# A two-layer gated parallel encoder on one core: order of the first loads, padded probabilities in D0, weight loads issued from the Pool queue

## The chip, the core and the metric

The kernel runs on one core of one Trainium2 chip. The core has a matrix engine (TensorE, "PE" in the rows; its weight loads are "PEld"), a vector engine (DVE), a scalar engine (ACT), GpSimd (POOL) and a sync engine (SP), each with an instruction queue of its own that is worked off in order. DMAs are issued by instructions in these queues and run on 16 DMA engines. The metric is the time of one execution in device microseconds; lower is better.

## What is computed

512 tokens of width 1024 go through two layers. Each layer normalises its input, projects it with one wide matrix, runs four attention branches (A: window with sink, B: differential, C: dense with rotary positions, D: three dilated groups), gates each branch, projects it back, mixes the four with sigmoid weights and adds the result to its input:

```python
for l in range(DEPTH):
    h = _rmsnorm(x, norm_gain[l])
    p = _project(h, w_in[l])                     # a_q, a_k, ..., d_v, gate, merge
    ...
    oa = _window_sink_attention(qa, ka, va, bias_a, sink[l]...)
    ob = _diff_attention(qb, kb, vb, tbl_b, lam, lam_init, sub_norm_gain[l])
    oc = _dense_gqa(qc, kc, vc)
    od = _dilated_attention(qd, kd, vd, bias_d)  # groups (128,1), (512,4), (2048,16)
    for n, o in enumerate((oa, ob, oc, od)):
        gated = o * silu(gate[n])
        merged += sigmoid(merge[n]) * (gated @ w_branch[l, n])
    x = x + merged @ w_out[l]
```

## The kernel before

Every float32 product is made from two float16 halves: an operand is split into a high part (`..h`, `whi`, `ph`, made on ACT) and a low part (`..l`, `wlo`, `pl`, made on DVE from the operand and the high part), and three matmuls (high by high, high by low, low by high) add up in PSUM.

The weights lie in DRAM as 132 pieces of 1 MB in the order in which they are used (`ORDER`). `dma_w` (L118) brings a piece as two loads of 128 x 1024 float32 into staging buffers `wst` (three of them), `load_w` splits it into one of four `whi`/`wlo` pairs (L142 on ACT, L143 on DVE), and `take_w` keeps three pieces ahead (`AHEAD`). A piece feeds 48 matmuls of 512 columns (`proj_n`, L396 to L398; `proj_t`, L407 to L409).

A layer is a chain of attention generators, each woven (`weave`) with the projections of what comes next. An attention step has `scores` (products `s`, L560 and L561; the bias is added on DVE into `t`; exponential and split into `ph`, `pl`) and `values` (products `pv`, L565 to L567). Tiles come from pools with a fixed number of buffers per tag, and a scheduler that replays the program on a timeline of its own fixes the order of each engine's queue when the kernel is built.

Opening of the program: `load_x` brings four blocks of 128 tokens (`xt`), `norm_a` normalises a block, `norm_b` transposes it on TensorE and splits it into `hT_h`, `hT_l`. The fourth block goes through `norm_t` instead, which splits first and transposes by two DMAs. `bias_lines` (L260) makes the relative-position bias of all heads: a matmul of the table `rb` with the one-hot matrix `oh` (97 x 2432), copied into `acc` rows 0 to 7 (L276, L278), and then one DMA on SP writes 23 copies of these 8 rows to `lines` in DRAM (L929). `load_bias` reads skewed tiles back from `lines` before each attention; the first of them are `bias_a`.

In group 0 of branch D (`attn_d0`, L801) a block of 128 keys meets only 256 queries, 64 on either side, so `ph` and `pl` hold 256 columns per key block and `values` multiplies them in pieces: 64-query halves (`lo`, `hi`) and, for the two middle blocks, one 128-query piece; 12 groups of three matmuls per head.

Of the kernel before, what the change touches and what calls it, by code (L numbers as in the profile page):

```python
# [85 lines left out]
)  # L86
PIECE = 128 * 2048
AHEAD = 3


@with_exitstack
def encoder(ctx, tc, x, wf, norm_gain, qk_gain, sink, lambda_vec, sub_gain, rel_bias, onehot, rope, out):
# [83 lines left out]
    def load_x(src, tt):  # L176
        if tt % 2 == 0:
            x_sb[tt // 2] = qk.tile([128, 2, D], F32, tag="qx", name="xt", bufs=2)
        nc.sync.dma_start(out=x_sb[tt // 2][:, tt % 2, :], in_=src[tt * 128:tt * 128 + 128, :])

    gain_b = {}

# [16 lines left out]
    load_x(x, 0)  # L199
    load_gain(0)  # L200
    dma_w(0)
    load_x(x, 1)
    with tc.issue_after(dma_w(1).ins):
        load_x(x, 2)
        nc.sync.dma_start(out=rb, in_=bass.AP(tensor=rel_bias.tensor, offset=rel_bias.offset, ap=[[0, 3], [36, 32], [1, 36]]))
        nc.sync.dma_start(out=oh, in_=onehot)
        load_x(x, 3)

    def norm_a(l, tt):

        xt = x_sb[tt // 2][:, tt % 2, :]
        ss = sm.tile([128, 2], F32, tag="n_ss", name="ss")
        for j in range(2):
            sq = tmp.tile([128, 512], F32, tag="sq", name="sq")
            S.activation(sq, xt[:, 512 * j:512 * j + 512], AF.Square, accum_out=ss[:, j:j + 1])
        V.tensor_tensor(ss[:, 0:1], ss[:, 0:1], ss[:, 1:2], op=ALUa)
        ln = sm.tile([128, 1], F32, tag="n_ln", name="ln")
        S.activation(ln, ss[:, 0:1], AF.Ln, scale=1.0 / D, bias=eps_x)
        rs = sm.tile([128, 1], F32, tag="n_rs", name="rs")
        S.activation(rs, ln, AF.Exp, scale=-0.5)  # L220
        hs = []
        for j in range(2):
            f = slice(512 * j, 512 * j + 512)
            h = tmp.tile([128, 512], F32, tag="gs", name="h", bufs=4)
            V.scalar_tensor_tensor(h, xt[:, f], rs, gain_b[l][:, f], op0=ALUm, op1=ALUm)
            hs.append(h)
        return hs

    def norm_b(tt, hs):

        for j in range(2):
            tr = transpose4(hs[j])
            d = slice(4 * j, 4 * j + 4)
            c = slice(tt * 128, tt * 128 + 128)
            S.activation(hT_h[:, d, c], tr, AF.Copy, scale=SH)
            done = V.scalar_tensor_tensor(hT_l[:, d, c], tr, SH, hT_h[:, d, c], op0=ALUm, op1=ALUs)
        return done

    def norm_t(tt, hs):

        hi = tmp.tile([128, 2, 512], F16, tag="st", name="h_hi", bufs=3)
        lo = tmp.tile([128, 2, 512], F16, tag="st", name="h_lo", bufs=3)
# [17 lines left out]
    def bias_lines():  # L260
# [3 lines left out]
        for a in (32, 64):  # L264
            r = slice(a, a + 32)
            V.tensor_tensor(rb[r, :], rb[r, :], rb16[r, :], op=ALUs)
            V.tensor_copy(rb16[r, :], rb[r, :])
        V.tensor_tensor(rb16[64:96, :], rb[64:96, :], rb16[64:96, :], op=ALUs)
        for i, (s0, ln_, h0, nh, off, w) in enumerate(SEG.values()):
            for e in range(0, ln_, 512):  # L270
                n = min(512, (ln_ + 1 - e))
                c = slice(s0 + e, s0 + e + n)
                p = ps_mm.tile([128, 512], F32, tag="mm", name="p")
                PE.matmul(p[:8, :n], rb16[:, h0:h0 + 8], oh[:, c], start=True, stop=True)
                if i % 2:
                    S.activation(accf[0:8, c], p[:8, :n], AF.Copy, scale=1.0 / SB)  # L276
                else:
                    V.tensor_scalar(accf[0:8, c], p[:8, :n], 1.0 / SB, None, op0=ALUm)  # L278
# [165 lines left out]
    def proj_q(res, l, kind, col, perm=False):  # L444
# [4 lines left out]
        for tt in range(NT):  # L449
# [9 lines left out]
            st = tmp.tile([128, 4, 4, HD], F16, tag="st", name="st", bufs=3)  # L459
# [10 lines left out]
    def proj_k(res, l, kind, col, perm=False):  # L470
# [6 lines left out]
        for tt in range(NT):  # L477
            p = proj_n(w, tt, perm, 512)
            rs_of(p, 8, out_ap=rsk[:, tt, :])
            kg = tmp.tile([128, 512], F32, tag="qn", name="kg")  # L480
            V.tensor_tensor(heads(kg), heads(p), tabs[l][:, n:n + 1, :].to_broadcast([128, 8, HD]), op=ALUm)
            st = tmp.tile([128, 16, 128], F16, tag="st", name="st", bufs=3)
            hi = st[:, 0:8, 0:HD]
            S.activation(hi, heads(kg), AF.Copy, scale=KS)
            V.scalar_tensor_tensor(st[:, 8:16, 0:HD], heads(kg), KS, hi, op0=ALUm, op1=ALUs)
            V.tensor_copy(st[:, :, HD:128], st[:, :, 0:HD])
            nc.sync.dma_start_transpose(out=kk[:, :, tt * 128:tt * 128 + 128], in_=st.rearrange("p a d -> p (a d)"))
            yield

    VS = SV / PROJ  # L490
# [20 lines left out]
    def proj_kv(res, l, kind, col):  # L511
# [6 lines left out]
        for tt in range(NT):  # L518
# [7 lines left out]
            st = tmp.tile([128, 4, 128], F16, tag="st", name="st", bufs=3)  # L526
# [270 lines left out]
    def attn_d0(l, qs, kk, rsk, v):  # L797
        bias, o, n12 = {}, {}, {}

        def scores(h):  # L800
            if h % 4 == 0:  # L801
                bias[h // 4] = load_bias("D0", h, 4, "bias_d0")
            ph, pl = new_p()
            for kb in range(4):
                q0, q1 = max(128 * kb - 64, 0), min(128 * kb + 192, T)
                n, f0 = q1 - q0, q0 - (128 * kb - 64)
# [2 lines left out]
                s_mm(p, kk[:, h, ks], kk[:, 8 + h, ks], qs[:, h, q0:q1])  # L809
                t = at.tile([128, 512], F32, tag="t", name="t", bufs=3)[:, :n]  # L810
                V.scalar_tensor_tensor(t, p, rsk[:, kb, h:h + 1], bias[h // 4][:, h % 4, f0:f0 + n], op0=ALUm, op1=ALUa)  # L811
                f = slice(f0, f0 + n)
                probs(t, n, nm[:, l, 12 + h:13 + h], ph[:, kb, f], pl[:, kb, f])
            return ph, pl

        def values(h, pp):
# [6 lines left out]
                                  in_=dsc[2][hp].rearrange("(t p) e -> p t e", p=128))  # L823
            pv = ps_pv.tile([128, 4, 66], F32, tag="pv", name="pv")
            for qb in range(4):
                vt = [v[:, k, h] for k in range(4)]
                lo, hi = pv[0:64, qb, 0:65], pv[64:128, qb, 0:65]
                if qb > 0:
                    k = qb - 1
                    pv_mm(lo, ph[:, k, 192:256], pl[:, k, 192:256], vt[k], HD, True, False)  # L830
                if qb < 3:
                    k = qb + 1
                    pv_mm(hi, ph[:, k, 0:64], pl[:, k, 0:64], vt[k], HD, True, False)
                if qb == 0:
                    pv_mm(lo, ph[:, 0, 64:128], pl[:, 0, 64:128], vt[0], HD, True, True)
                    pv_mm(hi, ph[:, 0, 128:192], pl[:, 0, 128:192], vt[0], HD, False, True)
                elif qb == 3:
                    pv_mm(lo, ph[:, 3, 64:128], pl[:, 3, 64:128], vt[3], HD, False, True)
                    pv_mm(hi, ph[:, 3, 128:192], pl[:, 3, 128:192], vt[3], HD, True, True)
                else:  # L840
# [74 lines left out]
    for l in range(L):  # L915
# [5 lines left out]
        if l:  # L921
            norm_t(3, last)
        else:
            bias_lines()
            with tc.issue_after(normed.ins):
                gain_tables(0)
        run(qa, proj_kv(r, l, "A", 512))
        if l == 0:
            nc.sync.dma_start(out=lines.rearrange("c h n -> h c n"),  # L929
                              in_=accf[0:8, 0:LINE].unsqueeze(1).to_broadcast([8, COPIES, LINE]))  # L930
            with tc.issue_after(normed.ins):
                setup_columns()
                setup()
        weave(attn_a(l, r["qA"], *r["kA"], r["vA"]),
# [90 lines left out]
```

## Time and profile before

| | us |
|---|---|
| time before, median of 3 runs | 1674.26 (1674.24 to 1674.72) |
| the profiled execution, own time | 1674.46 |
| its span, first to last instruction | 1672.4 |
| outside the span | 2.1 |
| mean granted TensorE clock over the span | 0.985 of 2.4 GHz |

The page of the profile gives busy time per engine; the rows that the prediction rests on stand two sections below. A busy PE means that some matmul is in flight: matmuls overlap, so the time that one costs is read from the distance between two starts in the timeline, not from its duration. DVE and ACT instructions overlap a little at their ends too, so that busy time in a window is less than the sum of durations.

### The profile page before, as it was taken

What the parts mean: (1) busy time and instruction counts of PE and PEld (TensorE: products, weight loads), DVE (VectorE), ACT (ScalarE), POOL (GpSimd) and SP (SyncE); (2) the same over time, 40 slices, a digit from 0 to 9 for tenths busy, and PEclk for the clock granted to TensorE, in tenths of its full rate; (3) what the DMA queues carried; (4) which work ended last, traced back from release to release, by engine and by line L of the source; (5) the groups of instructions that cost most, each with busy time, mean ns of one, the idle gap of its engine ahead of it and who ended that gap; (6) DMA issues with size and microseconds to landing.
All of it is one profiled execution on the core that took longest, in us unless ns stands there. A gap on an engine that the chain in (4) does not pass through costs nothing.

```text
span 1672.4 us, 26438 instructions
## 1 busy us (share of the span) xinstructions
PE 1602.6 (96%) x10302; PEld 834.6 (50%) x10302; DVE 1075.9 (64%) x2104; ACT 961.0 (57%) x1771; POOL 8.8 (1%) x32
## 2 busy tenths in 40 slices
PE   3389999999999999999999999999999999999999
PEld 1155545564555554454445554556455555445444
DVE  3368866785576766575556887678457676657451
ACT  3157676566664656564545767556667464556450
POOL 1000000000000000000000000000000000000000
PEclk8699999999999999999999999999999999999999
DMA  5974733352356757435357483336235674753421
GB/s 188 97 161 133 164 109 95 100 133 76 110 121 155 183 144 191 141 114 143 109 169 173 105 183 119 93 101 133 76 98 130 152 180 132 200 146 94 133 88 51
DMA packets 230817, 218.37 MB, mean 131 GB/s; under 512 B 176316, under 2 KB 188620, under 8 KB 230509
## 3 DMA queue, kind: packets, MB, share of 16 engines
q1 hardware_dynamic: 229925, 214.26, 50.0%
q0 software_dynamic: 768, 2.43, 0.5%
q8 instruction: 80, 1.31, 0.3%
q14 instruction: 44, 0.36, 0.1%
HBM read 163.94 MB, written 10.24 MB: 104 GB/s over the span
## 4 chain that ended last, share of the span: by engine, by line
PE 89%; DMA 6%; DVE 3%; ACT 1%; issue 0%; SPq 0%; DVEq 0%; ACTq 0%
PE mm L396 15%; PE mm L397 15%; PE mm L398 15%; PE mm L407 10%; PE mm L409 10%; PE mm L408 10%; PE s L560 3%; PE s L561 3%; PE pv L565 3%; DMA hT_h<-h_hi 2%; PE pv L567 2%; PE pv L566 2%; DMA oh<-in_onehot_dram 1%; DMA wst<-in_wf_dram 1%; DMA qs<-st 1%; DVE wlo L143 1%
## 5 line engine op out<-in xcount | busy, mean ns | idle before, releaser
L396 PE MATMUL mm<-whi,hT_h 128*128 128x512 f16 (+1 forms) x1408 | 522.7, 371 | 38.7 <-DMA hT_h<-h_hi 31.1
L397 PE MATMUL mm<-wlo,hT_h 128*128 128x512 f16 (+1 forms) x1408 | 522.6, 371 | 0.7 <-DVE wlo L143 0.7
L398 PE MATMUL mm<-whi,hT_l 128*128 128x512 f16 (+1 forms) x1408 | 522.2, 371 | 1.2 <-DMA hT_l<-h_lo 1.2
L143 DVE SCALAR_TENSOR_TENSOR wlo<-wst,whi 128x1024 f16<-128x1024 f32 (+1 forms) x260 | 307.3, 1204 | 203.1 <-ACT whi L142 202.0
L142 ACT ACTIVATE whi<-wst 128x1024 f16<-128x1024 f32 (+1 forms) x260 | 262.6, 1036 | 269.4 <-PE mm L408 122.3
L396 PEld LDWEIGHTS <-hT_h 128*128 128x128 f16 x1408 | 144.4, 103 | 175.9 <-DMA hT_h<-h_hi 32.1
L398 PEld LDWEIGHTS <-hT_l 128*128 128x128 f16 x1408 | 144.4, 103 | 147.6 <-issue 2.6
L397 PEld LDWEIGHTS <-hT_h 128*128 128x128 f16 x1408 | 144.4, 103 | 146.4 <-issue 7.7
L407 PE MATMUL mm<-hT_h,whi 128*128 128x512 f16 x512 | 194.1, 379 | 0.0
L409 PE MATMUL mm<-hT_h,wlo 128*128 128x512 f16 x512 | 194.1, 379 | 0.0
L408 PE MATMUL mm<-hT_l,whi 128*128 128x512 f16 x512 | 194.0, 379 | 0.0
L551 ACT ACTIVATE t<-t,nm 128x512 f32<-128x512 f32 (+2 forms) x224 | 132.0, 599 | 69.1 <-DVE t L811 24.1
L556 DVE TENSOR_TENSOR pl<-t,ph 128x512 f16<-128x512 f32 (+2 forms) x224 | 119.1, 543 | 37.8 <-ACT ph L555 36.5
L565 PE MATMUL pv<-v,ph 128*128 128x65 f16 (+2 forms) x992 | 123.8, 202 | 0.1
L566 PE MATMUL pv<-v,ph 128*128 128x64 f16 (+2 forms) x992 | 122.9, 201 | 0.0
L567 PE MATMUL pv<-v,pl 128*128 128x65 f16 (+2 forms) x992 | 121.0, 199 | 0.0
L409 PEld LDWEIGHTS <-wlo 128*128 128x128 f16 x768 | 75.1, 98 | 88.9
L407 PEld LDWEIGHTS <-whi 128*128 128x128 f16 x768 | 75.1, 98 | 87.1
L408 PEld LDWEIGHTS <-whi 128*128 128x128 f16 x768 | 75.1, 98 | 86.6
L555 ACT ACTIVATE ph<-t 128x512 f16<-128x512 f32 (+2 forms) x224 | 110.9, 506 | 2.8 <-PE pv L567 0.7
L560 PE MATMUL s<-qs,kk 128*128 128x512 f16 (+4 forms) x384 | 99.4, 293 | 1.7 <-DVE gs L582 1.3
L561 PE MATMUL s<-qs,kk 128*128 128x512 f16 (+4 forms) x384 | 100.5, 292 | 0.0
(173 smaller groups left out, 1925.4 us busy)
## 6 DMA issues: line engine op xcount, KB each, us to landing
wst<-in_wf_dram SPq DMA_DIRECT2D x264, 512.0 KB
dsc<-num SPq DMA_DIRECT2D x16, 260.0 KB
xt<-in_x_dram SPq DMA_DIRECT2D x8, 512.0 KB
bias_b<-lines SPq DMA_DIRECT2D x8, 448.0 KB
bias_a<-lines SPq DMA_DIRECT2D x16, 192.0 KB
num<-dsc SPq DMA_DIRECT2D x8, 260.0 KB
n<-dsc SPq DMA_DIRECT2D x8, 260.0 KB
bias_d<-lines SPq DMA_DIRECT2D x32, 64.0 KB
```

The source lines that it names most:

```text
L142: S.activation(hi[:, a], st[:, e:e + step], AF.Copy if sc is SW else AF.Identity, scale=sc)
L143: V.scalar_tensor_tensor(lo[:, a], st[:, e:e + step], sc, hi[:, a], op0=ALUm, op1=ALUs)
L396: PE.matmul(p[:, :ncol], a, wh, start=(k == 0), stop=False)
L397: PE.matmul(p[:, :ncol], a, wl, start=False, stop=False)
L398: PE.matmul(p[:, :ncol], b, wh, start=False, stop=(k == 7))
L407: PE.matmul(p, wh[:, k, f], rh[:, k], start=(k == 0), stop=False)
L408: PE.matmul(p, wh[:, k, f], rl[:, k], start=False, stop=False)
L409: PE.matmul(p, wl[:, k, f], rh[:, k], start=False, stop=(k == nk - 1))
L561: PE.matmul(p, klo, q, start=False, stop=True)
L565: PE.matmul(o, ph, vt[:, 0:d + 1], start=start, stop=False)
L566: PE.matmul(o[:, 0:d], ph, vt[:, d + 2:2 * d + 2], start=False, stop=False)
L567: PE.matmul(o, pl, vt[:, 0:d + 1], start=False, stop=stop)
```

## The change

Three things are done together.

First, the opening. SP issues only the four `xt` blocks and the gain; the first weight pieces go out beside them. `rb` and `oh` are loaded later and from Pool, behind a small Pool copy (`there`) that waits for the fourth `xt` block. All four blocks take `norm_b`. `bias_lines` moves behind the key and value projection of branch A; its matmul has each head's column repeated 16 times (`rbr`), so that the bias lands in all 128 rows of `acc` (16 copies of 8 heads), and two DMAs from Pool, of 128 and of 56 rows, write the 23 copies.

Second, D0. `ph` and `pl` hold 384 columns per key block, with 64 zeroed columns on either side (four Pool memsets per head), and `values` uses 128-query pieces alone, as branch A does: 10 groups of three matmuls per head.

Third, the weights. `dma_w` issues on Pool (`nc.gpsimd`), and there are five `wst` buffers. The staging tag `st` gets four buffers, and `proj_k` splits its tile and its transposing DMA in two.

```diff
+WST = 5
@@ dma_w
-            st = wp.tile([128, 1024], F32, tag="wst", name="wst", bufs=3)
-            dma = nc.sync.dma_start(out=st, in_=src[:, e:e + 1024])
+            st = wp.tile([128, 1024], F32, tag="wst", name="wst", bufs=WST)
+            dma = nc.gpsimd.dma_start(out=st, in_=src[:, e:e + 1024])
@@ first loads
-    load_x(x, 1)
-    with tc.issue_after(dma_w(1).ins):
-        load_x(x, 2)
-        nc.sync.dma_start(out=rb, in_=...)
-        nc.sync.dma_start(out=oh, in_=onehot)
-        load_x(x, 3)
+    dma_w(1)
+    for tt in range(1, NT):
+        load_x(x, tt)
+    there = const.tile([128, 1], F32, name="there")
+    tables = G.tensor_copy(there, x_sb[1][:, 1, 0:1])
@@ bias_lines
+        rbr = const.tile([97, len(SEG), 128], F16, name="rbr")
+            V.tensor_copy(rbr[:, i].rearrange("p (c h) -> p c h", h=8),
+                          rb16[:, h0:h0 + 8].unsqueeze(1).to_broadcast([97, 16, 8]))
-                PE.matmul(p[:8, :n], rb16[:, h0:h0 + 8], oh[:, c], start=True, stop=True)
+                PE.matmul(p[:, :n], rbr[:, i], oh[:, c], start=True, stop=True)
-                    S.activation(accf[0:8, c], p[:8, :n], AF.Copy, scale=1.0 / SB)
+                    S.activation(accf[:, c], p[:, :n], AF.Copy, scale=1.0 / SB)
+        for c0, c1_ in ((0, 16), (16, COPIES)):
+            nc.gpsimd.dma_start(out=lines[c0:c1_]..., in_=accf[0:8 * (c1_ - c0), 0:LINE])
     for tt in range(NT):
-        normed = (norm_b if tt < 3 else norm_t)(tt, norm_a(0, tt))
-        if tt < 2:
-            load_w(tt)
+        normed, split = norm_b(tt, norm_a(0, tt))
+        if tt == 0:
+            with tc.issue_after(scaled[0].ins):
+                load_w(0)
+            with tc.issue_after(split.ins):
+                load_w(1)
@@ proj_k
-            st = tmp.tile([128, 16, 128], F16, tag="st", name="st", bufs=3)
+            st = [tmp.tile([128, 8, 128], F16, tag="st", name="st", bufs=4) for _ in range(2)]
...
+            for i in range(2):
+                V.tensor_copy(st[i][:, :, HD:128], st[i][:, :, 0:HD])
+                nc.sync.dma_start_transpose(out=kk[:, 8 * i:8 * i + 8, ...], in_=st[i]...)
@@ attn_d0 scores
+            for pp in (ph, pl):
+                G.memset(pp[:, :, 0:64], 0.0)
+                G.memset(pp[:, :, 320:384], 0.0)
-                f = slice(f0, f0 + n)
+                f = slice(f0 + 64, f0 + 64 + n)
@@ attn_d0 values
-                if qb > 0:
-                    pv_mm(lo, ph[:, k, 192:256], pl[:, k, 192:256], vt[k], HD, True, False)
...
-                    pv_mm(pv[:, qb, 0:65], ph[:, qb, 64:192], pl[:, qb, 64:192], vt[qb], HD, False, True)
+                kbs = [k for k in (qb - 1, qb, qb + 1) if 0 <= k < 4]
+                for kb in kbs:
+                    f = slice((qb - kb + 1) * 128, (qb - kb + 2) * 128)
+                    pv_mm(pv[:, qb, 0:65], ph[:, kb, f], pl[:, kb, f], v[:, kb, h], HD, kb == kbs[0], kb == kbs[-1])
@@ first layer, behind the projections of branch A
-            nc.sync.dma_start(out=lines.rearrange("c h n -> h c n"), in_=accf[0:8, 0:LINE]...to_broadcast([8, COPIES, LINE]))
+            bias_lines()
```

In the queue of SP, at the start of the program, there stood before (`lines<-acc` is the bias write, `hT_h<-h_hi` the fourth block's transpose):

```order
L179 DMA xt<-in_x_dram 128x1024
L205 DMA rb<-in_rel_bias_dram 96x1x36
L206 DMA oh<-in_onehot_dram 97x2432
L179 DMA xt<-in_x_dram 128x1024
L125 DMA wst<-in_wf_dram 128x1024 x3
L929 DMA lines<-acc 8x23x2432
L125 DMA wst<-in_wf_dram 128x1024 x3
L247 DMA_TRANSPOSE hT_h<-h_hi 128x8x128
```

Now the same loads stand in the queue of Pool, from its 14th instruction on; SP has only the `xt` blocks, the gain and then transposes:

```order
L126 DMA wst<-in_wf_dram 128x1024 x5
L514 MEMSET v 128x8
L514 MEMSET v 128x16
L126 DMA wst<-in_wf_dram 128x1024
L208 COPY there<-xt 128x1
L377 DMA gb<-in_qk_gain_dram 128x512
L379 DMA rope_t<-in_rope_dram 128x512
L931 DMA rb<-in_rel_bias_dram 96x1x36
L933 DMA oh<-in_onehot_dram 97x2432
L322 DMA rbb<-in_rel_bias_dram 128x576
L126 DMA wst<-in_wf_dram 128x1024 x2
```

The one-hot load stands behind all four `xt` blocks instead of ahead of the fourth, six weight loads stand ahead of it and the others behind it.

On DVE, just ahead of the first bias add of branch A (`t<-s,rsk,bias_a`), there stood before:

```order
L143 SCALAR_TENSOR_TENSOR wlo<-wst,whi 128x1024
L529 SCALAR_TENSOR_TENSOR st<-kg,st 128x2x64
L496 SCALAR_TENSOR_TENSOR v<-mm,v 128x2x64
L359 SCALAR_TENSOR_TENSOR nlam<-le 128x1 x2
L530 COPY st<-st 128x4x64
L653 SCALAR_TENSOR_TENSOR t<-s,rsk,bias_a 128x256
```

and now:

```order
L144 SCALAR_TENSOR_TENSOR wlo<-wst,whi 128x1024
L284 TENSOR_SCALAR acc<-p 128x384
L543 SCALAR_TENSOR_TENSOR st<-kg,st 128x2x64
L510 SCALAR_TENSOR_TENSOR v<-mm,v 128x2x64
L371 SCALAR_TENSOR_TENSOR nlam<-le 128x1 x2
L284 TENSOR_SCALAR acc<-p 128x256
L544 COPY st<-st 128x4x64
L596 SCALAR_TENSOR_TENSOR gs<-mm,sig 128x512
L667 SCALAR_TENSOR_TENSOR t<-s,rsk,bias_a 128x256
```

The copies of the bias (`acc<-p`) stood some 75 instructions earlier in that queue before; now the last of them is three instructions ahead of the first add that needs the bias back from DRAM.

## Rows read from the trace of the kernel before

**Rows 1.** The page: span, and busy time, share and instructions of two engines

```profile
span 1672.4 us, 26438 instructions
PE 1602.6 (96%) x10302; PEld 834.6 (50%) x10302; DVE 1075.9 (64%) x2104; ACT 961.0 (57%) x1771; POOL 8.8 (1%) x32
```

**Rows 2.** Windows: stretch, length, busy us (instructions) per engine, PE clock, DMA share, GB/s

```profile
0.00:114.65 114.65, 54.45 (x259) 28.38 (x260) 50.10 (x119) 38.48 (x97) 5.74 (x20) 0.78 0.78 155
0.00:131.60 131.60, 70.14 (x335) 35.72 (x336) 60.85 (x139) 52.36 (x124) 5.74 (x20) 0.81 0.73 145
131.60:870.00 738.40, 736.83 (x4825) 383.88 (x4824) 493.01 (x956) 442.48 (x795) 2.23 (x8) 1.00 0.50 132
870.00:910.00 40.00, 37.04 (x218) 20.97 (x216) 27.55 (x52) 22.77 (x56) 0.00 (x0) 1.00 0.84 204
910.00:1660.00 750.00, 749.93 (x4891) 390.28 (x4889) 493.14 (x957) 443.36 (x799) 0.85 (x4) 1.00 0.47 124
```

**Rows 3.** Waits of PE: who waited for whom, us in total, times, longest

```profile
PE mm L396 <- DMA hT_h<-h_hi: 31.1, 2, 30.2
PE p L274 <- DMA oh<-in_onehot_dram: 15.3, 1, 15.3
```

**Rows 4.** Timeline of SP's queue: start, length, engine, line, DMA

```profile
13.82 0.40 SPq L206 DMA_DIRECT2D oh<-in_onehot_dram  x1
...
44.25 0.31 SPq L929 DMA_DIRECT2D lines<-acc  x1
...
56.13 25.60 SPq L247 DMA_TRANSPOSE hT_h<-h_hi  x1
```

**Rows 5.** Windows, three stretches of the opening, columns as in rows 2

```profile
10.00:16.00 6.00, 4.31 (x10) 1.32 (x11) 3.75 (x6) 4.34 (x9) 0.00 (x0) 1.00 1.02 378
30.00:38.00 8.00, 0.00 (x0) 0.00 (x0) 0.00 (x0) 0.00 (x0) 0.00 (x0) 0.50 0.06 26
65.00:80.00 15.00, 0.00 (x0) 0.00 (x0) 0.00 (x0) 0.00 (x0) 0.00 (x0) 0.50 0.47 65
```

**Rows 6.** Windows, the first 23.75 us, columns as in rows 2

```profile
0.00:11.70 11.70, 1.95 (x9) 1.58 (x9) 2.61 (x5) 4.81 (x11) 4.67 (x18) 1.00 0.83 265
11.70:23.75 12.05, 9.60 (x32) 3.48 (x33) 9.23 (x22) 8.37 (x21) 0.00 (x0) 1.00 0.68 237
```

**Rows 7.** Timeline: the first bias add of branch A on DVE

```profile
114.65 1.00 DVE L653 SCALAR_TENSOR_TENSOR t<-s,rsk,bias_a 128x256 f32<-128x256 f32 x2
```

**Rows 8.** One tile loaded by Pool: issue ns min/median/max, first and last start; landing

```profile
L367 POOL DMA_DIRECT2D rope_t<-in_rope_dram x2: 537/537/537, 2.2 to 755.6; - x2
...
DMA to landing us min/median/max: 7.1/7.9/8.8
```

**Rows 9.** The page's DMA issues: the weight loads and the size of each

```profile
wst<-in_wf_dram SPq DMA_DIRECT2D x264, 512.0 KB
```

**Rows 10.** Groups on Pool by shape: busy us, mean ns of one, idle before, releasers

```profile
L500 POOL MEMSET v<- 128x32 f16 x6 | 1.4, 239 | 719.6 <-PE pv L567 636.1 <-DVE gs L582 83.5
```

**Rows 11.** Timeline of PE around one head's values of branch A, then of D0

```profile
131.38 0.38 PE L398 MATMUL mm<-whi,hT_l 128*128 128x512 f16 x1
131.60 0.19 PE L565 MATMUL pv<-v,ph 128*128 128x65 f16 x1
...
132.51 0.27 PE L560 MATMUL s<-qs,kk 128*128 128x256 f16 x1
...
704.67 0.23 PE L565 MATMUL pv<-v,ph 128*64 128x65 f16 x2
...
704.95 0.19 PE L567 MATMUL pv<-v,pl 128*64 128x65 f16 x1
705.07 0.20 PE L565 MATMUL pv<-v,ph 128*128 128x65 f16 x1
705.11 0.20 PE L566 MATMUL pv<-v,ph 128*128 128x64 f16 x1
...
705.99 0.26 PE L560 MATMUL s<-qs,kk 128*128 128x192 f16 x1
```

More of the change, by code (lines that the diff above doesn't have):

```diff
@@ L178, in load_x @@
             x_sb[tt // 2] = qk.tile([128, 2, D], F32, tag="qx", name="xt", bufs=2)
-        nc.sync.dma_start(out=x_sb[tt // 2][:, tt % 2, :], in_=src[tt * 128:tt * 128 + 128, :])
+        return nc.sync.dma_start(out=x_sb[tt // 2][:, tt % 2, :], in_=src[tt * 128:tt * 128 + 128, :])
     gain_b = {}
@@ L201, in encoder @@
     dma_w(0)
-    load_x(x, 1)
-    with tc.issue_after(dma_w(1).ins):
-        load_x(x, 2)
-        nc.sync.dma_start(out=rb, in_=bass.AP(tensor=rel_bias.tensor, offset=rel_bias.offset, ap=[[0, 3], [36, 32], [1, 36]]))
-        nc.sync.dma_start(out=oh, in_=onehot)
-        load_x(x, 3)
+    dma_w(1)
[3 more added lines that the diff above has]
+    tables = G.tensor_copy(there, x_sb[1][:, 1, 0:1])
+    scaled = [None]
     def norm_a(l, tt):
@@ L234, in norm_b @@
             c = slice(tt * 128, tt * 128 + 128)
-            S.activation(hT_h[:, d, c], tr, AF.Copy, scale=SH)
+            split = S.activation(hT_h[:, d, c], tr, AF.Copy, scale=SH)
             done = V.scalar_tensor_tensor(hT_l[:, d, c], tr, SH, hT_h[:, d, c], op0=ALUm, op1=ALUs)
-        return done
+        return done, split
     def norm_t(tt, hs):
-        hi = tmp.tile([128, 2, 512], F16, tag="st", name="h_hi", bufs=3)
-        lo = tmp.tile([128, 2, 512], F16, tag="st", name="h_lo", bufs=3)
+        hi = tmp.tile([128, 2, 512], F16, tag="st", name="h_hi", bufs=4)
+        lo = tmp.tile([128, 2, 512], F16, tag="st", name="h_lo", bufs=4)
         for j in range(2):
@@ L273, in bias_lines @@
                 p = ps_mm.tile([128, 512], F32, tag="mm", name="p")
-                PE.matmul(p[:8, :n], rb16[:, h0:h0 + 8], oh[:, c], start=True, stop=True)
+                PE.matmul(p[:, :n], rbr[:, i], oh[:, c], start=True, stop=True)
                 if i % 2:
-                    S.activation(accf[0:8, c], p[:8, :n], AF.Copy, scale=1.0 / SB)
+                    S.activation(accf[:, c], p[:, :n], AF.Copy, scale=1.0 / SB)
                 else:
-                    V.tensor_scalar(accf[0:8, c], p[:8, :n], 1.0 / SB, None, op0=ALUm)
+                    V.tensor_scalar(accf[:, c], p[:, :n], 1.0 / SB, None, op0=ALUm)
+        for c0, c1_ in ((0, 16), (16, COPIES)):
+            nc.gpsimd.dma_start(out=lines[c0:c1_].rearrange("c h n -> (c h) n"), in_=accf[0:8 * (c1_ - c0), 0:LINE])
     for tt in range(NT):
-        normed = (norm_b if tt < 3 else norm_t)(tt, norm_a(0, tt))
-        if tt < 2:
-            load_w(tt)
+        normed, split = norm_b(tt, norm_a(0, tt))
[4 more added lines that the diff above has]
+                load_w(1)
     maxb = const.tile([128, 36], F32, name="maxb")
@@ L481, in proj_k @@
             V.tensor_tensor(heads(kg), heads(p), tabs[l][:, n:n + 1, :].to_broadcast([128, 8, HD]), op=ALUm)
-            st = tmp.tile([128, 16, 128], F16, tag="st", name="st", bufs=3)
-            hi = st[:, 0:8, 0:HD]
+            st = [tmp.tile([128, 8, 128], F16, tag="st", name="st", bufs=4) for _ in range(2)]
+            hi = st[0][:, :, 0:HD]
             S.activation(hi, heads(kg), AF.Copy, scale=KS)
-            V.scalar_tensor_tensor(st[:, 8:16, 0:HD], heads(kg), KS, hi, op0=ALUm, op1=ALUs)
-            V.tensor_copy(st[:, :, HD:128], st[:, :, 0:HD])
-            nc.sync.dma_start_transpose(out=kk[:, :, tt * 128:tt * 128 + 128], in_=st.rearrange("p a d -> p (a d)"))
+            V.scalar_tensor_tensor(st[1][:, :, 0:HD], heads(kg), KS, hi, op0=ALUm, op1=ALUs)
+            for i in range(2):
+                V.tensor_copy(st[i][:, :, HD:128], st[i][:, :, 0:HD])
+                nc.sync.dma_start_transpose(out=kk[:, 8 * i:8 * i + 8, tt * 128:tt * 128 + 128],
+                                            in_=st[i].rearrange("p a d -> p (a d)"))
             yield
@@ L923, in encoder @@
         else:
-            bias_lines()
-            with tc.issue_after(normed.ins):
+            with tc.issue_after(normed.ins), tc.issue_after(tables.ins):
                 gain_tables(0)
+                nc.gpsimd.dma_start(out=rb, in_=bass.AP(tensor=rel_bias.tensor, offset=rel_bias.offset,
+                                                        ap=[[0, 3], [36, 32], [1, 36]]))
+                nc.gpsimd.dma_start(out=oh, in_=onehot)
         run(qa, proj_kv(r, l, "A", 512))
         if l == 0:
-            nc.sync.dma_start(out=lines.rearrange("c h n -> h c n"),
-                              in_=accf[0:8, 0:LINE].unsqueeze(1).to_broadcast([8, COPIES, LINE]))
-            with tc.issue_after(normed.ins):
+            bias_lines()
+            with tc.issue_after(normed.ins), tc.issue_after(tables.ins):
                 setup_columns()
```

21 lines of the change are left out of this document (4 added, 17 removed).

## The prediction, made before the changed kernel was run

> **What bounds the kernel now.** I read the page first: PE is busy for 1602.6 of 1672.4 us [rows 1], so 69.8 us of PE idle time are all that any reordering can win; what is left must come out of PE's own work. Then the windows, to see where the idle time lies [rows 2]. Up to 131.60 us PE is busy for 70.14 us, so 61.5 us of the 69.8 are lost in the opening. From there to 870 us it loses 1.6 us, at the border of the layers (870 to 910 us) 3.0 us, in the 750 us behind it 0.07 us. So there are two regimes: an opening that waits, and a body that is bound by PE alone, where no load, no split and no transpose ends last.
>
> Third, PE's waits, for what ends last in the opening [rows 3]: 30.2 us in one piece for `hT_h`, the fourth block's transpose by DMA, and 15.3 us for `oh`. The timeline of SP's queue gives the causes [rows 4]. `oh` is issued at 13.82 us. While PE waits for it, the DMA share is 0.06 at 26 GB/s [rows 5], one sixteenth: one DMA engine carries it alone, and the fourth `xt` block, issued behind it, waits too. Then the write of `lines`, issued at 44.25 us, moves at 65 GB/s [rows 5], against 378 GB/s when the first loads run [rows 5], and the transpose of the fourth block sits behind it: its issue alone holds SP for 25.60 us [rows 4].
>
> As a mark for the end of the opening I take the first values product of branch A, at 131.60 us [rows 11]. Ahead of it PE has the same 96 query matmuls, 96 key and value matmuls of 256 columns and 96 gate matmuls in both kernels, so the time of this mark is the gain.
>
> **The opening after the change.** The fourth block no longer passes through a DMA transpose, and all `xt` blocks and five weight loads, 5 MB, go first. At 378 GB/s that is 13 us. So the 30.2 us wait has nothing left to wait for, and the 15.3 us wait too, as far as `oh` comes before it is needed. What is late next?
>
> PE could be through with its part by 70.14 us of busy time (which has some slow-clock stretches in it) plus the 7.7 us that it must wait for the first block, 78 us. DVE is later in one place. Up to its first bias add at 114.65 us it has 50.10 us of work [rows 2, 7], which the change moves about and hardly shrinks (five small copies to `rbr` are new, about 1 us). In the first 23.75 us, while the first blocks arrive, it is busy for 2.61 + 9.23 us and idle for 11.9 [rows 6]. I keep that idle time, since the blocks arrive at the same pace. So DVE can be at the bias add at 62 us. But now the last copy of the bias into `acc` stands right ahead of this add on DVE, and between the two lie the write to `lines` and the read of `bias_a`, which before had 70 us of slack [rows 4, 7]. All else on DVE is queued behind that add. The write is 23 x 8 x 2432 x 4 bytes = 1.79 MB. Price of write and read together: 4.7 us (1.79 MB at 378 GB/s) and the shorter read, 0.5 us, are the floor, 5.7 us with the issue of 0.54 us [rows 8]; two landings of 8.8 us [rows 8] and the 4.7 us are the ceiling, 22 us. I take 12 us, nearer the floor, because the write now leaves from 128 rows. Bias add: 62 + 12 = 74 us.
>
> From the add to the mark took 17 us before (114.65 to 131.60) [rows 7, 11]. In that time PE still had most of the 96 gate matmuls to do. In the new order 68 of them stand ahead of PE's first product that needs a bias result, so they run while DVE waits. 28 are left, at 0.22 us from start to start [rows 11] 6.2 us. Floor 6.2, ceiling 17; I take 10 us, because the last of four key blocks must still pass DVE, ACT and DVE. Mark: 84 us. **Gain 131.6 - 84 = 47.5 us.** By the bounds the mark lies between 78 us (PE alone) and 62 + 22 + 17 = 101 us, the gain between 53.6 and 30.6 us.
>
> **D0's values.** One head of branch A, 30 matmuls in 10 groups of one shape, takes 132.51 - 131.60 = 0.91 us; one head of D0, 36 matmuls in 12 groups, takes 705.99 - 704.67 = 1.32 us [rows 11]. The extra is not only the six matmuls. In a group, starts are 0.03 to 0.04 us apart (705.07, 705.11), but from the last 64-column matmul to the next 128-column one 0.12 us (704.95 to 705.07), so each change of shape costs about 0.09 us. The new D0 has branch A's form: 0.41 us less per head, 16 heads, 6.6 us. Two heads per layer are split up by other matmuls and change shape more often, so I put 7 us. D0 lies where PE has no idle time [rows 2], so all of it counts. **Gain 7 us.** The new memsets take 0.24 us each [rows 10], 64 of them 15 us in two layers, on an engine that is busy for 8.8 us [rows 1]. Each waits until the values two heads earlier have let the buffer go. Queued behind it on Pool are the next two weight loads. Cover: a piece lasts PE 48 x 0.22 = 10.6 us, and three pieces are kept ahead. Without that cover a late pair of loads would cost PE up to one piece, 10.6 us.
>
> **Weight loads on Pool.** 264 issues [rows 9] leave SP and come to Pool at 0.54 us each [rows 8], 142 us out of 1670. The rates needed do not change: 0.5 MB per 5.3 us. Gain: 1.6 + 3.0 us of PE idle time behind the opening, at most, if SP's transposes no longer stand behind a weight load that waits for its buffer. I put 0, since the waits there are not shown to be SP's. Loss: the body is bound by PE as long as a load lands in under 5.3 us on average; that is the rival below. Extra `st` and `wst` buffers and the two halves of `proj_k`'s transposes cost no instruction on PE. I put 0, covered by DVE and SP, neither of which ends last in the body.
>
> One rule speaks against this part. The Trainium skill (SBUF — State Buffer, "SBUF: two separate sides") says that a DMA issued by GpSimd stalls while DVE runs a two-port operation, because its descriptors cannot be written. Pool's issue took 537 ns both at 2.2 us, with DVE not yet at work [rows 6], and at 755.6 us, in the body [rows 8], so here no row shows such a stall.
>
> **Sum.** 1674.26 - 47.5 - 7 = 1619.8, **1620 us**. The profiled execution took 1674.46 us, 0.2 us over the median, so the median is the base. With the gain's bounds this case reaches from 1613 to 1637 us.
>
> **Rivals.**
>
> (a) *`oh` still travels on one DMA engine.* It has 97 rows as before, 472 KB, 18 us at 26 GB/s [rows 5]. Issued at about 20 us it lands at 38. In Pool's queue the loads of the fourth piece stand behind it, and on DVE the split of that piece stands ahead of the last half block of `hT_l` and of all query work. DVE would come there at about 31 us and wait 7 to 8 us. Time: 1620 + 8 = 1628 us, 1621 to 1645 with the same bounds. For it: the same shape. Against it: another queue makes the descriptors. The Trainium skill (DMA: Bandwidth & Descriptors, "Why a DMA increments its semaphore by 16 and not by 1") has a DMA use the largest number of engines up to 16 that divides its rows, one for a prime such as 97, and reports that loads issued by GpSimd were seen to spread such rows over nearly all engines. The 0.06 of rows 5 agrees with the first half; the second half no row here shows, and by it this rival falls.
>
> (b) *The opening is bound by PE*, because the bias comes back as fast as the floor says and DVE idles less than 11.9 us. Mark 78 us: 1674.3 - 53.6 - 7 = 1613.7; with the 3 us of the layer border 1611 us.
>
> (c) *Pool's queue delays PE in the body:* a memset or an early Pool copy holds weight loads back in D0 or in the opening, a few us per place. With 10 us in two or three places 1640 to 1650 us.
>
> (d) *Slower: the weight loads become the bound.* Pool's loads of 256 KB took 7.1 to 8.8 us to land [rows 8]. If 512 KB took 7.1 us each and one at a time, 264 x 7.1 = 1874 us. It decides from 1674 / 264 = 6.3 us per load on. Against it: five buffers let five loads be under way, and both queues together moved 265 GB/s in the first 11.7 us [rows 6], where the body needs 100.
>
> (e) *No change:* the wait for `hT_h` is replaced by an equally long one for the bias. The path at its ceiling is 22 us, not 47, so this needs two errors at once; 1670 to 1677 us.
>
> **How the numbers follow.** A measurement of this kernel can tell about 0.2%, 3.3 us, from no change. Chances: forecast (1613 to 1637) 0.55, (a) 0.18, (b) 0.10, (c) 0.10, (d) 0.05, (e) 0.02. Faster: the forecast, (a), (b) and (c), 0.93; same 0.02; slower 0.05. The range takes in the forecast, (a) nearly whole and (b)'s upper part: 1610 to 1642 us; outside are (c), (d), (e) and the ends of (a) and (b), together under 0.2.
>
> **What would show it.** Right: the first values product of branch A at 78 to 101 us; no PE wait for `hT_h` or `oh` over 2 us in the opening; DVE's longest wait in it is for `bias_a`; a D0 head of 30 matmuls in 0.91 us; PE without idle time behind the mark. (a) would show as a stretch with a DMA share of 0.06 and DVE waiting for a split. (d) and (c) would show as PE waiting for `wlo` or `whi` in the body, ACT waiting for `wst`, or Pool waiting in D0 with loads behind it. The forecast is wrong if the mark lies later than 101 us, or if PE loses more than 5 us behind it.

## The result, and the profile of the changed kernel

The changed kernel takes 1630.46 us (median of four executions, 1626.05 to 1630.65), the kernel before 1674.25 beside it: ratio 0.9732, 95% interval [0.9715, 0.9748]. It is faster by 43.8 us. The prediction said 1620, in a range of 1610 to 1642: the time lies in the range, 10 us above the forecast.

The page of the changed kernel, against [rows 1] and [rows 9]: PE is busy for 98% of the span, the weight loads stand on Pool's queue and land 5.0 us after their issue (median).

```profile
span 1628.8 us, 26582 instructions
...
PE 1591.9 (98%) x10214; PEld 834.0 (51%) x10214; DVE 1073.9 (66%) x2141; ACT 957.2 (59%) x1771; POOL 169.8 (10%) x365
...
wst<-in_wf_dram POOLq DMA_DIRECT2D x264, 512.0 KB, 5.0
```

Where the 43.6 us between the two spans come from is read by cutting both at the same products: the first values product of branch A, D0's first and last whole head, the first values product of the second layer's branch A, the end. The windows of the kernel before (stretch, length, busy us and instructions per engine, PE clock, DMA share, GB/s), whose first stretch is in [rows 2]:

```profile
131.60:704.67 573.07, 571.50 (x3802) 303.91 (x3800) 395.28 (x766) 356.30 (x640) 0.98 (x5) 1.00 0.52 133
704.67:766.88 62.21, 62.21 (x517) 32.68 (x517) 46.53 (x122) 37.86 (x80) 1.07 (x2) 1.00 0.47 134
766.88:929.54 162.66, 159.70 (x822) 77.65 (x822) 91.46 (x146) 85.70 (x162) 0.17 (x1) 1.00 0.51 140
929.54:1672.40 742.86, 739.04 (x4833) 384.62 (x4831) 481.81 (x935) 428.76 (x767) 0.85 (x4) 1.00 0.47 124
```

The same five stretches of the changed kernel:

```profile
0.00:86.50 86.50, 67.39 (x343) 36.39 (x344) 56.55 (x138) 48.57 (x118) 18.82 (x44) 0.94 0.74 222
86.50:660.42 573.92, 571.80 (x3801) 304.20 (x3800) 398.40 (x788) 358.36 (x647) 53.47 (x107) 1.00 0.54 133
660.42:718.01 57.59, 57.59 (x476) 31.84 (x474) 44.80 (x120) 37.49 (x80) 11.72 (x34) 1.00 0.50 145
718.01:891.07 173.06, 161.50 (x816) 77.91 (x815) 92.86 (x148) 85.66 (x162) 16.06 (x31) 0.97 0.51 131
891.07:1628.80 737.73, 733.65 (x4785) 383.66 (x4783) 481.26 (x951) 427.15 (x768) 69.78 (x149) 1.00 0.47 124
```

| stretch | before | after | gain |
|---|---|---|---|
| opening, to the first values product of A | 131.60 | 86.50 | 45.1 |
| A to D0 of the first layer | 573.07 | 573.92 | -0.85 |
| D0, first to last whole head | 62.21 | 57.59 | 4.6 |
| end of D0, border of the layers, to the second A | 162.66 | 173.06 | **-10.4** |
| second layer, with its D0 | 742.86 | 737.73 | 5.1 |

So the opening gave about what it should and D0 somewhat more, and the border of the layers took 10.4 us back. There PE was idle for 11.6 us (173.06 - 161.50) instead of 3.0, and its own work took 1.8 us longer. PE's waits between 700 and 880 us in the changed kernel (total, times, longest):

```profile
PE mm L408 <- DMA hT_h<-h_hi: 7.3, 1, 7.3
PE mm L410 <- DMA hT_l<-h_lo: 2.8, 1, 2.8
PE mm L408 <- DVE qn L470: 1.2, 1, 1.2
```

They are for the DMA transposes that turn the second layer's input, blocks of 128 x 1024 float16. The chain of waits, from 826 us on, names the one that ends last:

```profile
828.19 1.21 DVE h_lo L248 x2
...
829.46 15.06 DMA hT_l<-h_lo
...
844.57 0.61 PE mm L410
```

Beside the transposes Pool has issued four weight loads within 5.3 us, as its timeline shows:

```profile
823.16 0.53 POOL L126 DMA_DIRECT2D wst<-in_wf_dram  x1 [16.18 <-DVE wlo L144]
...
828.49 0.53 POOL L126 DMA_DIRECT2D wst<-in_wf_dram  x1 [0.61 <-DVE wlo L144]
```

The last two land after 11.9 us instead of 5.0, by the DMA issues from 826 to 840 us (KB each, median us to landing):

```profile
wst<-in_wf_dram POOLq DMA_DIRECT2D x2, 512.0 KB, 11.9
```

Two windows of the changed kernel: loads without transposes (one store of the layer's output goes beside them), and then loads and transposes together, where the rate is lowest.

```profile
803.00:812.00 9.00, 9.00 (x44) 4.05 (x42) 5.86 (x9) 4.22 (x10) 1.58 (x3) 1.00 0.80 272
830.00:836.00 6.00, 3.46 (x17) 1.37 (x14) 2.84 (x6) 2.78 (x8) 0.00 (x0) 1.00 1.26 78
```

The busy share of the DMA engines is higher in the second row (1.26), but they move 78 GB/s, under a third of the first. And while PE waits, its clock falls. Windows of the changed kernel around the wait:

```profile
826.00:833.00 7.00, 7.00 (x34) 3.20 (x33) 6.52 (x11) 3.29 (x11) 1.06 (x2) 1.00 1.06 214
833.00:841.00 8.00, 0.74 (x4) 0.13 (x2) 0.56 (x2) 1.35 (x3) 0.00 (x0) 0.81 1.11 162
841.00:846.00 5.00, 2.19 (x6) 0.59 (x5) 3.10 (x6) 1.23 (x4) 0.00 (x0) 0.50 1.15 196
846.00:856.00 10.00, 10.00 (x50) 4.97 (x48) 2.14 (x4) 2.26 (x6) 0.00 (x0) 0.89 0.24 49
```

After 7.3 us of idle time PE works at 0.50 (1.2 GHz) until about 848 us. There lie the 1.8 us of longer work.

### The profile page after: what moved, and what is told of

Same layout as the page of the kernel before. It is cut to its first block, busy times and chain, and to the rows that moved or that the text cites. A ratio compares the mean times of both kernels' runs of the same rounds, so it can differ in the third digit from the quotient of the medians.

```text
span 1628.8 us, 26582 instructions
## 1 busy us (share of the span) xinstructions
PE 1591.9 (98%) x10214; PEld 834.0 (51%) x10214; DVE 1073.9 (66%) x2141; ACT 957.2 (59%) x1771; POOL 169.8 (10%) x365
## 4 chain that ended last, share of the span: by engine, by line
PE 90%; DVE 4%; DMA 4%; issue 1%; ACT 1%; SPq 0%; POOL 0%; DVEq 0%; ACTq 0%; POOLq 0%
PE mm L408 17%; PE mm L410 16%; PE mm L409 16%; PE mm L421 10%; PE mm L419 10%; PE mm L420 10%; PE s L574 3%; PE s L575 3%; PE pv L580 2%; PE pv L581 2%; PE pv L579 2%; DVE wlo L144 1%; DMA hT_l<-h_lo 1%; DMA qs<-st 1%; DMA xt<-in_x_dram 1%
## 5 line engine op out<-in xcount | busy, mean ns | idle before, releaser
L143 ACT ACTIVATE whi<-wst 128x1024 f16<-128x1024 f32 (+1 forms) x260 | 256.7, 1034 | 145.4 <-PE mm L420 120.3
L126 POOL DMA_DIRECT2D wst<-in_wf_dram x264 | 141.4, 536 | 1297.0 <-DVE wlo L144 1228.1
L580 PE MATMUL pv<-v,ph 128*128 128x64 f16 (+1 forms) x960 | 118.4, 201 | 0.0
L579 PE MATMUL pv<-v,ph 128*128 128x65 f16 (+1 forms) x960 | 118.4, 200 | 0.0
L581 PE MATMUL pv<-v,pl 128*128 128x65 f16 (+1 forms) x960 | 116.7, 199 | 0.0
L574 PE MATMUL s<-qs,kk 128*128 128x512 f16 (+4 forms) x384 | 99.7, 293 | 4.2 <-DMA kk<-st 3.5
```

Source lines behind the costliest of these rows:

```text
L143: S.activation(hi[:, a], st[:, e:e + step], AF.Copy if sc is SW else AF.Identity, scale=sc)
L574: PE.matmul(p, khi, q, start=True, stop=False)
L579: PE.matmul(o, ph, vt[:, 0:d + 1], start=start, stop=False)
L580: PE.matmul(o[:, 0:d], ph, vt[:, d + 2:2 * d + 2], start=False, stop=False)
L581: PE.matmul(o, pl, vt[:, 0:d + 1], start=False, stop=stop)
```

## Experiments

Ratios are to the kernel before on the same chip. Their intervals are about 0.0015 to 0.0024 either way, so that by an estimate from them the difference of two ratios is known to some 4 us. A trace shows one execution; the traces of the first kernel below, of D0's values as before and of the later set-up are of executions 3.5 to 4.9 us under the medians of their kernels.

### Why the border lost 10 us: four kernels

Theory: loads on Pool's queue and transposes on SP's queue share the DMA engines and slow each other down. Rivals: it is the fourth and fifth buffer (more loads at once), or SP's own chain, with no part for the loads. The first kernel puts the loads back on SP's queue, with five buffers:

```diff
-            dma = nc.gpsimd.dma_start(out=st, in_=src[:, e:e + 1024])
+            dma = (nc.gpsimd if i < 10 else nc.sync).dma_start(out=st, in_=src[:, e:e + 1024])
```

> The changed kernel with its weight loads from the eleventh piece on issued by SP again; five buffers and all else kept. Where the missing gain went: between D0's last head and the second layer's branch A the changed kernel needs 173.1 us, the kernel before 162.7. Theory (two queues): loads on Pool's queue and transposes on SP's share the DMA engines packet by packet and both crawl; on one queue they follow each other. Expected: that stretch back to 162 to 165 us, 1630.5 - 9 = 1619 to 1624 us, as long as SP's transposes behind waiting loads cost PE nothing elsewhere. Rival 1 (depth): the fourth and fifth buffer put more loads on the DMA engines at the border, whatever their queue: 1627 to 1632 us. Rival 2 (SP's own chain: the writes of the second layer's input and the st buffers hold the transposes, loads play no part): 1629 to 1632 us.

The second keeps Pool's queue, with three buffers (`WST = 3`):

> The changed kernel with three weight buffers instead of five, loads still on Pool. Two queues: the loads are issued as each buffer comes free, so they still meet the border's transposes: 1628 to 1634 us, stretch from D0's last head to the second branch A 168 to 175 us. Rival 1 (depth): 1619 to 1624 us, stretch 162 to 165 us. Rival 2: 1629 to 1632 us. If three buffers on Pool are too few to cover a load, PE waits for weight splits in the body as well.

The third takes the collision away and leaves the queues: the loads of two pieces wait for the last transpose.

```diff
             norm_t(3, last)
+            gate = const.tile([128, 1], F16, name="gate")
+            held[71] = held[72] = G.tensor_copy(gate, hT_l[:, 7, 511:512])
...
+            if i in held:
+                with tc.issue_after(held[i].ins):
+                    dma = nc.gpsimd.dma_start(out=st, in_=src[:, e:e + 1024])
```

> The changed kernel; the four loads of pieces 71 and 72, which ran at 824 to 841 us beside the border's transposes, wait on Pool until the last of these transposes has landed. Two queues and rival 1 (both: the loads slow the transposes): the pair of transposes of the third block lands in 3 to 4 us instead of 15, PE's wait there falls from 7.3 + 2.8 to under 3 us, 1619 to 1624 us. Rival 2: no change, 1629 to 1632 us.

The fourth takes the DMA transposes away (`norm_b` for `norm_t` at both places of the border):

> The changed kernel; at the border of the layers all four blocks are turned by PE, as in the opening, instead of by DMA. It adds 32 products of 0.11 us from start to start, 3.5 us of PE work. If the wait for the transposes is the whole loss of the border (10.4 us more than before in the stretch from D0's last head to branch A), 1630.5 - 10.8 + 3.5 = 1623 us, 1621 to 1626. If the loss comes from somewhere else (PE waits for residuals, splits or weights there), 1630 to 1635 us.

Measured: 1626.70 us (0.9719 [0.9704, 0.9733]), 1631.76 (0.9744 [0.9721, 0.9768]), **1619.11 (0.9674 [0.9660, 0.9689])** and 1621.20 (0.9692 [0.9678, 0.9707]). The stretch from D0's last head to the second branch A, one window of each kernel in the same order, against 173.06 and 162.66:

```profile
715.36:883.87 168.51, 161.22 (x815) 78.06 (x814) 93.19 (x147) 85.93 (x162) 0.17 (x1) 0.98 0.48 135
```

```profile
719.09:891.97 172.88, 161.43 (x815) 78.00 (x814) 91.28 (x146) 85.45 (x162) 16.05 (x31) 0.97 0.51 131
```

```profile
719.38:879.45 160.07, 158.76 (x816) 77.61 (x815) 92.41 (x147) 85.80 (x162) 16.23 (x32) 1.00 0.51 142
```

```profile
718.22:881.85 163.63, 162.57 (x847) 81.18 (x846) 92.69 (x148) 85.20 (x162) 16.07 (x31) 1.00 0.45 126
```

Without the collision the stretch is shorter than in either original, and PE waits 1.3 us in it. The timeline of SP's queue in the held-loads kernel shows the third and the fourth block's transposes. One load of Pool is left beside the first of them, issued at 824.10 us and landed 4.1 us later:

```profile
827.32 1.54 SPq L255 DMA_TRANSPOSE hT_h<-h_hi  x1
...
837.04 1.25 SPq L255 DMA_TRANSPOSE hT_l<-h_lo  x1
```

The fourth block's last one is through within 3.8 us of its issue, when the Pool copy that waits for it runs (Pool's timeline of the same kernel):

```profile
840.81 0.19 POOL L934 COPY gate<-hT_l 128x1 f16<-128x1 f16 x1 [16.18 <-DMA hT_l<-h_lo]
```

So the loads are the cause; SP's own chain falls. Buffers alone fall too: with three on Pool nothing changed. But the first kernel missed: on one queue with five buffers its trace has 4.5 of the 10.4 us back, and the ratios 2.2 us, which is not clear of noise. Neither the queue nor the depth alone brings the stretch back; the next kernel changes both.

### One part undone or done alone: three kernels

Loads as before from the eleventh piece on (SP's queue, three buffers), the rest as changed:

```diff
-WST = 5
+WST = 3
...
+            dma = (nc.gpsimd if i < 10 else nc.sync).dma_start(out=st, in_=src[:, e:e + 1024])
```

> The changed kernel with the weight loads as in the kernel before from the eleventh piece on: SP's queue and three buffers; opening and D0 as changed. If the weight part of the change is what costs the border its 10.4 us: the stretch from D0's last head to the second branch A comes back to 161 to 165 us (162.7 before, 173.1 changed, 168.5 with SP and five buffers), 1618 to 1622 us. Rival: the border is lost because the shorter opening and D0 move the loads against the transposes, so that the kernel before was lucky: 168 us or more, 1626 to 1632 us.

Measured: 1621.94 us, 0.9683 [0.9667, 0.9700], as expected. The border's stretch:

```profile
719.84:882.76 162.92, 159.26 (x815) 77.41 (x814) 92.63 (x147) 85.46 (x162) 0.17 (x1) 1.00 0.53 139
```

The kernel before was not lucky: its loading gives 162.9 us in the new surroundings too. The weight loads' new queue and depth, as far as they act behind the opening, cost (0.9732 - 0.9683) x 1674 = **8.2 us** (the `st` buffers and the halved transposes of `proj_k` were left as changed). Border by queue and buffers: SP with three 162.9, SP with five 168.5, Pool with three 172.9, Pool with five 173.1.

The kernel before with only the weight loads moved (`nc.sync` to `nc.gpsimd` in `dma_w`):

> The kernel before with one edit: its weight loads issued by Pool instead of SP, still three buffers. The prediction put 0 for this move, a gain of 4.6 us at most: 1670 to 1675 us. If loads on a queue of their own slow the border's transposes in this kernel too: 1677 to 1686 us, with PE waiting 5 to 11 us for hT_h or hT_l at 870 to 910 us. If SP's loads had been holding up the opening's transposes: below 1668 us.

Measured: 1692.01 us, 1.0104 [1.0088, 1.0121], slower by 17 us, more than expected. The border shows a like loss, 8.1 us over 162.66:

```profile
774.62:945.40 170.78, 161.40 (x821) 77.93 (x821) 91.85 (x147) 85.44 (x162) 16.10 (x31) 0.98 0.49 133
```

Another 6.9 us come from the opening (first values product of A at 138.47 instead of 131.60), which no theory had. PE's waits of this kernel, against [rows 3]:

```profile
PE mm L396 <- DMA hT_h<-h_hi: 31.4, 2, 29.2
PE mm L396 <- ACT whi L142: 19.9, 2, 17.9
PE mm L398 <- DMA hT_l<-h_lo: 11.0, 2, 6.5
```

The wait for `oh` has turned into one of 17.9 us for `whi`: ACT stands in the fourth block's normalisation, waiting 18.4 us for its `xt`, which on SP still follows `oh`. ACT's waits up to 60 us:

```profile
ACT sq L215 <- DMA xt<-in_x_dram: 23.0, 3, 18.4
```

What makes the opening longer by 6.9 us in sum was not taken apart.

D0's values as before, in the changed kernel:

> The changed kernel with D0's values as before: 64-column products, no padding, no memsets. The prediction's price of this part was 7 us: 1637.5 us, 1636 to 1639. By the two traces it is 10.1 us (from D0's first head to the end of its last 5.05 us less per layer, since the step into a head's first 64-column product, 0.10 us more than in the new form, was left out of the 0.41 us): 1640.5 us, 1639 to 1642.

Measured: 1640.89 us, 0.9794 [0.9778, 0.9810]: (0.9794 - 0.9732) x 1674 = 10.4 us. The ratios alone would not tell this from the prediction's 7; the traces do. Between the first and the last whole head of the first layer this kernel takes 61.77 us against 57.59, and from the second branch A to the end 743.0 against 737.7: 4.2 + 5.3 = 9.5 us, beside 4.6 + 5.1 between the two originals. PE's timeline at the step from a merge product into a D0 head, first of the kernel before, whose head begins at 704.67 [rows 11]:

```profile
704.36 0.38 PE L409 MATMUL mm<-gT,wlo 128*128 128x512 f16 x1
```

Then of the changed kernel, with the end of that head:

```profile
660.21 0.38 PE L421 MATMUL mm<-gT,wlo 128*128 128x512 f16 x1
660.42 0.19 PE L579 MATMUL pv<-v,ph 128*128 128x65 f16 x1
...
661.34 0.24 PE L574 MATMUL s<-qs,kk 128*128 128x192 f16 x1
```

The head takes 0.92 us instead of 1.32, and the step into it 0.21 instead of 0.31.

### What sets the mark of the opening: two kernels and a base

The bias path is lengthened by a second write of the lines behind the first:

```diff
-        for c0, c1_ in ((0, 16), (16, COPIES)):
+        for c0, c1_ in 2 * ((0, 16), (16, COPIES)):
```

> The changed kernel; the bias lines are written twice, one write behind the other, so the first bias add of branch A comes about 8 us later (77.1 to about 85 us). The prediction's path (DVE, write, read, add, mark) sets the mark: first values product at 94 to 95 us, as much later as the add. PE's own work with its waits sets it, and the bias path has 1.5 us of slack (the last split that this product needs ended 1.5 us ahead of it): 93 us. PE's work alone with ample slack: 86.5 us, unchanged.

Measured, one execution: 1631.99 us. On DVE's timeline the last copy of the bias and the first bias add of the changed kernel, then the add of this one:

```profile
62.75 0.41 DVE L284 TENSOR_SCALAR acc<-p 128x256 f32<-128x256 f32 x1
...
71.95 0.69 DVE L596 SCALAR_TENSOR_TENSOR gs<-mm,sig 128x512 f32<-128x512 f32 x1 [8.65 <-ACT sig L594]
77.13 1.53 DVE L667 SCALAR_TENSOR_TENSOR t<-s,rsk,bias_a 128x256 f32<-128x256 f32 x3 [4.48 <-DMA bias_a<-lines]
```

```profile
84.08 1.53 DVE L667 SCALAR_TENSOR_TENSOR t<-s,rsk,bias_a 128x256 f32<-128x256 f32 x3 [8.92 <-DMA bias_a<-lines]
```

And on PE's timeline the first values product of the longer path, against 86.50 us:

```profile
88.00 0.26 PE L579 MATMUL pv<-v,ph 128*128 128x65 f16 x1
```

The add comes 7.0 us later and the mark 1.5, only 3.9 us behind the add: in the changed kernel the bias path has some 5.5 us of slack, more than the 1.5 that I had read from the end of a split. With the longer path PE waits 2.7 us for the add; in the changed kernel it waits for nothing between the last bias copy and the mark, as its window shows (columns as above):

```profile
63.16:86.50 23.34, 23.34 (x106) 10.55 (x105) 6.76 (x16) 10.18 (x21) 1.07 (x2) 0.93 0.48 152
```

So the way of the bias to DRAM and back costs the changed kernel nothing. What PE waits for ahead of the mark is in its waits up to 90 us in the changed kernel:

```profile
PE tr L256 <- DVE h L228: 7.6, 1, 7.6
PE mm L408 <- DVE qn L470: 5.0, 2, 3.0
PE s L574 <- DMA kk<-st: 3.5, 3, 2.7
PE mm L408 <- ACT whi L143: 2.0, 1, 2.0
```

`qn` is late because the rope tables and the set-up of maxima and sinks stand ahead of it on DVE. On the held-loads kernel I moved them behind the last bias copy, where DVE idles (8.7 us from 63.3 us on), beside the held-loads kernel as it was:

```diff
-                gain_tables(0)
+                loaded = gain_tables(0)
...
+            copied = bias_lines()
+            with tc.issue_after(copied.ins):
+                rope_tables(0, *loaded)
-            with tc.issue_after(normed.ins), tc.issue_after(tables.ins):
+            with tc.issue_after(copied.ins), tc.issue_after(tables.ins):
                 setup_columns()
                 setup()
```

> The held-loads kernel, and on DVE the rope tables (2.3 us) and the set-up of maxima and sinks (about 6 us) queued behind the last copy of the bias into acc instead of ahead of the query and key work at 33 to 53 us. If DVE's lateness there (PE waits of 2.7 + 0.6 + 2.8 us for qn) sets the mark, and the bias path has slack: those waits fall to under 2 us in all, the mark comes at 80 to 84 us instead of 87, 1613 to 1616 us against 1619. If the opening is bound by the path of the bias (DVE, write, read, add): the last copy comes earlier on DVE, but the mark moves with the add only, 1616 to 1619 us. If the moved work now holds up the first adds or the first exponentials of branch A: 1619 us or more.

> The held-loads kernel once more, as the base for the one beside it: 1617 to 1621 us, PE without a wait over 2 us between 800 and 860 us.

Measured: **1614.17 us, 0.9631 [0.9616, 0.9646]**, and the base 1620.59, 0.9673 [0.9660, 0.9686]. The mark, on PE's timeline of the later set-up:

```profile
78.90 0.19 PE L589 MATMUL pv<-v,ph 128*128 128x65 f16 x1
```

PE's waits up to 82 us there:

```profile
PE s L584 <- DMA kk<-st: 2.8, 1, 2.8
PE mm L418 <- DVE qn L480: 1.9, 1, 1.9
```

The time came as expected and the mark earlier than the 80 to 84 us. In the base beside it the mark was at 90.0 us (87.0 in the first trace of that kernel), and PE waited 4.9 us for `qn`, 3.8 for `kk` and 2.3 for the bias add. The pair alone does not part DVE's order from the bias, because the bias comes forward too: the last copy ends at 57.8 us instead of 63.4, and the add stands at 70.4 instead of 80.1:

```profile
70.37 1.53 DVE L677 SCALAR_TENSOR_TENSOR t<-s,rsk,bias_a 128x256 f32<-128x256 f32 x3 [1.07 <-DMA bias_a<-lines]
```

But from that copy to the mark PE is busy throughout here as well:

```profile
57.77:78.90 21.13, 21.13 (x102) 9.87 (x101) 14.20 (x47) 10.04 (x22) 1.61 (x3) 1.00 0.50 156
```

So in the changed kernel and in this one PE's work and its earlier waits set the mark; in the base the bias add held PE up for 2.3 us besides. This kernel beats both originals.

## Why the prediction was right, and where it was wrong

**The opening: right in size, wrong on what ends last.** Forecast 47.5 us, measured 45.1; the mark came at 86.5 us, forecast 84. The terms were close: DVE was through with the last bias copy at 63.2 us (forecast 62), write and read took 14.0 us to the add (forecast 12), the add came 9.4 us ahead of the mark (forecast 10). But this path was not the one that PE waited for: all of PE's 19.1 us without work lie ahead of the end of the last bias copy. That the last term came out is luck, since with the add 7 us later 3.9 us were enough: the first values product needs the first key block, not the last of four. The step that failed is "DVE is later in one place": DVE was late for PE at 36 and 50 us already, for `qn`. PE's 67.4 us of work, 7.6 for the first block, 10.5 for `qn`, `kk` and `whi` and 1.0 of small waits are the 86.5. Rival (b) had the right bound, PE, without these waits; with the set-up moved the mark came at 78.9, its waits 4.2 us and its work 3.4 us shorter than in the changed kernel (granted clock 0.98 instead of 0.94). The forecast held because the path that I priced ended only some 5.5 us ahead of the one that binds, and that is luck too. One sign failed accordingly: DVE's longest wait in the opening was not for `bias_a` (4.5 us) but for a gate's sigmoid on ACT (8.7 us).

**The old waits.** `oh` and the fourth block's `hT_h` hold up nothing in the opening any more, as forecast. Rival (a) falls: `oh`, issued by Pool, landed after 6.2 us, where 472 KB at 26 GB/s [rows 5] would take 18. The half of the Trainium skill's rule (DMA: Bandwidth & Descriptors, "Why a DMA increments its semaphore by 16 and not by 1") that no row showed before, that loads by GpSimd spread such rows, agrees with this.

**D0: right mechanism, a term too small.** 7 us forecast, 10.4 measured. The term is the 0.41 us per head: it ran from the head's first product to the next score product, and so left out the change of shape on the way in, another 0.10 us. 8 whole heads at 0.51 us would be 4.1 us per layer, and the second layer gained 5.1 in all; that the rest comes from heads that are split up by other products and change shape more often than I allowed was not measured apart. The memsets cost PE nothing, as said.

**Weight loads on Pool: wrong, by 8.2 us.** The step that failed is "the rates needed do not change": 0.5 MB per 5.3 us holds on average, and by it five buffers are ample, but at the border four loads are issued within 6 us, beside transposes that PE needs at once. On SP's queue with three buffers the two were issued in turn, and the transposes that ended last took 5.6 and 5.9 us instead of 15.1; I took that order for a cost (a gain of up to 4.6 us when it goes) and never asked what it protected. How order and depth share in this protection is not shown beyond the four values above. [Rows 4] held a hint, a single transpose that kept SP for 25.60 us beside the write of the lines. The prediction's own test of being wrong, PE losing more than 5 us behind the mark, came true. That the time lies in the range all the same is no merit of this part: the range was taken from the bounds of the opening and from two rivals, and nothing in it stood for a loss at the border. Rival (c) had the size, about 10 us in one place, with another mechanism: no memset and no Pool copy was in it. The stall by DVE, cited from the Trainium skill, did not show in the time of an issue: 264 issues took 536 ns on average and 833 at most, beside the 537 before [rows 8]; whether DVE ran a two-port operation beside one, no run here shows. Rival (d) did not come near: 5.0 us to landing, several loads at a time.

**Sum.** By the stretches 45.1 - 0.85 + 4.6 - 10.4 + 5.1 = 43.6 us between the spans; of the 0.85, 0.55 are waits (PE waits 0.7 and 1.4 us for DVE there, where it waited 1.6 before) and 0.3 longer work. Without the loss at the border the forecast of 1620 is met within 2 us: loads as before gave 1621.9, held loads 1619.1.

## What to carry to other kernels

Before a stream of loads is moved to a queue of its own, look at what its old queue kept apart: a queue in order is also a schedule. Price such a move at the places where transfers come in a burst, not by the average rate, and where one must go first, make the others wait for it. When a path is shortened, ask of each engine when it is late for the one that bounds, not only when it reaches the end.

## What the runs showed of the hardware

A DMA transpose and weight loads in flight together on two queues both crawl: a transpose of 128 x 1024 float16 took 15.1 us, where one without loads beside it was through within 3.8, and two loads took 11.9 us to land instead of 5.0. The Trainium skill (DMA: Bandwidth & Descriptors, "Queues, rings and completion order") has each DMA engine go round its queues packet by packet. A transpose that is held up by loads agrees with this. Such a sharing alone should leave the sum of the rates as it was. For 6 us it does not: 78 GB/s in sum, where loads without transposes moved 272. Over the 20 us from 826 to 846 it does: the windows above come to 189 GB/s (214, 162 and 196), and the same windows of the held-loads kernel, with 203, 175 and 199 GB/s, to 191. So PE lost its time by the order in which the bytes came, not by their number. What happens in the 6 us, no run here shows.

Two waits of PE of 7.3 and 2.8 us close together were followed by work at a granted clock of 0.50 (1.2 GHz) until about 848 us, which made the work of that stretch 1.8 us longer.

A change between products of 64 and of 128 columns costs PE about 0.1 us each time: 0.12 us from start to start instead of 0.03 to 0.04 inside a head [rows 11], and 0.31 instead of 0.21 on the way into one.
